# First phase without GpSimd, and adaLN steps issued between the blocks of the second product

## The chip, the cores and the metric

The kernel runs on one core of one Trainium2 chip. The metric is the device time of one launch in microseconds (us). Inputs lie in HBM, the output goes back to HBM, and all arithmetic runs on the core's engines: PE (TensorE), DVE (VectorE), ACT (ScalarE) and POOL (GpSimd). SP issues nearly all loads.

## What is computed

Two layers over 512 latent and 256 context tokens of width 1024. Each layer is a SwiGLU half step, a token mixer and a second SwiGLU half step. Before each of these comes an RMS norm with a shift and a scale, behind it a gate. Cut to what matters here:

```python
for i in range(2):
    mod_l = silu(c)     @ ada_w[i] + ada_b[i]     # 9 vectors of 1024: sh1,sc1,g1, sh2,sc2,g2, sh3,sc3,g3
    mod_c = silu(c_ctx) @ ada_w[i] + ada_b[i]     # the same for the context tokens
    x = x + 0.5 * g1 * swiglu(rms(x) * (1 + sc1) + sh1, pre_wi[i], pre_wo[i])
    x = x + g2 * mixer(rms(x) * (1 + sc2) + sh2)  # attention; layer 0 differential, layer 1 windowed
    x = x + 0.5 * g3 * swiglu(rms(x) * (1 + sc3) + sh3, post_wi[i], post_wo[i])
def swiglu(h, wi, wo):                            # 1024 -> 2 x 2816 -> 1024
    g, u = split(h @ wi); return (silu(g) * u) @ wo
```

The 18 adaLN vectors ("mods") are 18 x 1024 dot products of length 1024 for each of two token types. Their weights, ada_w, are 75 MB.

## The kernel before

Features lie on the 128 partitions, in 8 chunks (d or k); tokens lie on the free axis, 512 latent and 256 context. fp32 matrices are split into two parts, hi and lo (lines 72 to 74: ACT copies the hi part, DVE subtracts it), and each product is the sum of three.

**The four feed-forward steps** (function ffn). The hidden width is 22 slabs f. up(f) makes slab f of the hidden layer: for f = 0, 1, 2 with 8 plain products each (line 522), from f = 3 on with the seven products of a Strassen-Winograd step (line 456). For these, Seven.sums (T1, T2, T3 and their parts) first makes sums and differences of the normalised input (lines 420 to 430), beside up(1) and up(2). After every fourth slab down(g) multiplies four hidden slabs with the second matrix (line 569): 16 blocks, each ended by a DVE instruction that adds it into x (line 390). The last down ends with Norm.follow: squares, sums and the next norm, whose chunks (line 369 on) feed the next product.

**adaLN.** Shift and scale of the first norm (mods 0 and 1 of layer 0) are needed before anything else. For them ada_job reads a 512 KB slab of weights (araw) for each chunk; DVE multiplies and accumulates it for the latent tokens (line 187), POOL multiplies it for the context tokens (line 190) and ACT sums POOL's products (line 199). Four of the eight scale chunks go to PE instead (scale_job, line 215: the weights are the stationary side, 2 columns move). All other mods are made by class Halves in "steps": one step reads 128 x 512 weights (wh, three buffers) and has two accumulating DVE instructions (line 253), one for each type. ffn's hook `beside` issues 6, 4 or 5 of them after each up(f), in the first, second and third feed-forward step.

**Order.** The program is written for a scheduler that orders each engine's instructions beforehand by readiness and program order; keep() pins an instruction to its place in the program. On the chip each engine runs its list strictly in that order, SP its list of loads too.

Of the kernel before, what the change touches and what calls it, by code (L numbers as in the profile page):

```python
# [17 lines left out]
P = 128  # L18
# [24 lines left out]
def hybrid_backbone_kernel(ctx: ExitStack, tc: tile.TileContext, I, out):  # L43
# [74 lines left out]
    def ada_vectors(pool):  # L118

        crep = pool.tile([P, 2, D], F32, name="crep")  # L120
        for ty, nm in enumerate(("c", "c_ctx")):
            nc.sync.dma_start(crep[:, ty], I[nm].partition_broadcast(P))
            nc.scalar.activation(crep[:, ty], crep[:, ty], AF.Silu)
        nc.sync.dma_start(adab, I["ada_b"])
        return crep

    def load_x(half):
        s0, n, _, _ = half
        for d in range(0, KC, 4):
            nc.sync.dma_start(x[:, d:d + 4, s0:s0 + n], I["x"][:, d:d + 4, s0:s0 + n])  # L130
# [42 lines left out]
    JUNK, PRODS = 3, 3  # L173

    def ada_job(l, j, engines, pool, crep, bufs, pin=False):
        m, d = divmod(j, KC)
        w = pool.tile([P, D], F32, name="araw", tag="araw", bufs=bufs)
        nc.sync.dma_start(w, I["ada_w"][l, j])
        if mods[l][m] is None:
            md = const.tile([P, 2, KC], F32, name=f"mod{l}_{m}")  # L180
            mods[l][m] = md[:, 0], md[:, 1], md
        prods = []
        for ty in range(2):
            acc = mods[l][m][ty][:, d:d + 1]
            if engines[ty] is nc.vector:
                o = pool.tile([P, D], BF16, name="junk", tag="junk", bufs=JUNK)
                i = nc.vector.scalar_tensor_tensor(o, w, 1.0, crep[:, ty], ALU.mult, ALU.mult, accum_out=acc)
            else:
                pr = pool.tile([P, D], F32, name="aprod", tag="aprod", bufs=PRODS)
                i = nc.gpsimd.tensor_mul(pr, w, crep[:, ty])  # L190
                prods.append((pr, acc))
            if pin:
                keep(i)
        md = mods[l][m][2][:, :, d]

        def finish():
            for pr, acc in prods:
                o = pool.tile([P, D], BF16, name="junk", tag="junk", bufs=JUNK)
                nc.scalar.activation(o, pr, AF.Identity, accum_out=acc)
            bias = adab[:, l, j:j + 1].broadcast_to([P, 2])  # L200
            if m in (1, 4, 7):
                nc.vector.scalar_tensor_tensor(md, md, 1.0, bias, ALU.add, ALU.add)
            else:
                nc.vector.tensor_add(md, md, bias)
                if m in (2, 8):
                    nc.vector.tensor_scalar_mul(md, md, 0.5)
        return finish

    def scale_job(k, pool, bufs):

        w = pool.tile([P, D], F32, name="araw", tag="araw", bufs=bufs)
        nc.sync.dma_start(w, I["ada_s"][k])
# [3 lines left out]
        bias = adab[:, 0, KC + k:KC + k + 1].broadcast_to([P, 2])  # L216
        return lambda: nc.vector.scalar_tensor_tensor(mods[0][1][2][:, :, k], ps, 1.0, bias, ALU.add, ALU.add)

    class Halves:
# [6 lines left out]
        def add(self, l, ms):  # L226
# [9 lines left out]
            def silu(q):  # L236
                cs = []
                for nm in ("c", "c_ctx"):
                    t = small.tile([P, 512], F32, name="ch", tag="ar", bufs=3)
# [5 lines left out]
            def job(pool, q, m, d):  # L245
# [3 lines left out]
                w = pool.tile([P, 512], F32, name="wh", tag="wh", bufs=3)  # L249
# [11 lines left out]
            for q in range(2):  # L261
                for m in ms:
                    for d in range(KC):
                        def f(pool, q=q, m=m, d=d):
                            if q == 0 and d == 0:
                                bias(m)
                            if m == ms[0] and d == 0:
                                silu(q)
                            job(pool, q, m, d)
                        self.steps.append(f)  # L270

        def __call__(self, n, pool):
            for _ in range(min(n, len(self.steps))):
                self.steps.pop(0)(pool)
# [1007 lines left out]
```

## Time and profile before

| | |
|---|---|
| time, median of 3 runs | 2940.08 us (2938.19 to 2943.32) |
| profiled execution: its own time | 2939.59 us |
| its span, first to last instruction | 2937.8 us |
| PE busy | 2733.8 us (93%) |
| DVE busy | 2229.2 us (76%) |
| ACT busy | 1229.8 us (42%) |
| POOL busy | 498.3 us (17%) |
| mean granted TensorE clock | 0.979 of full |

The profile shows one execution. The time contains 1.8 us outside the span. A busy PE is an upper figure, because matmuls overlap in the records.

### The profile page before, as it was taken

Reading aid. Unit: us, or ns where it says so; the run is one execution under the profiler, and the core shown is the slowest. Engines: PE = TensorE matmul, PEld = TensorE weight load, DVE = VectorE, ACT = ScalarE, POOL = GpSimd, SP = SyncE. Lnnn points to the kernel's source line nnn. Section 1 sums busy time; section 2 is a strip of 40 time slices with the busy share of each in tenths; the row PEclk is TensorE's granted clock in tenths of the full one; section 3 lists DMA queues with packets and bytes.
Section 4 is the critical chain, followed back from the end, with each engine's and each line's share of the span. In section 5 each row is a group of like instructions: output and inputs, shape, how many; then the busy total and the mean of one; then the engine's idle time right before and its main releaser. Section 6 shows DMA issues by size and latency. Waiting matters only on the chain.

```text
span 2937.8 us, 47517 instructions
## 1 busy us (share of the span) xinstructions
PE 2733.8 (93%) x17948; PEld 2589.0 (88%) x17948; DVE 2229.2 (76%) x4613; ACT 1229.8 (42%) x3053; POOL 498.3 (17%) x586
## 2 busy tenths in 40 slices
PE   4799899999999989799999989999999999999999
PEld 3698898889999978789999978999998999999999
DVE  7988987877677756877886598787766766488887
ACT  4423222336556644323333343332334566454443
POOL 5300000025433422200000051000002521220000
PEclk9899999999999999899999999999999999999999
DMA  6333433322011022233332223343322101223333
GB/s 209 114 127 129 133 125 101 119 79 73 30 30 34 26 85 73 86 108 115 109 114 65 72 76 115 126 133 112 100 73 89 45 29 30 73 78 101 98 93 101
DMA packets 98709, 266.49 MB, mean 91 GB/s; under 512 B 12592, under 2 KB 16688, under 8 KB 98352
## 3 DMA queue, kind: packets, MB, share of 16 engines
q1 hardware_dynamic: 91968, 251.78, 26.8%
q10 hardware_dynamic: 6512, 11.68, 1.2%
q8 instruction: 141, 2.31, 0.3%
q14 instruction: 88, 0.72, 0.1%
HBM read 256.07 MB, written 7.34 MB: 90 GB/s over the span
## 4 chain that ended last, share of the span: by engine, by line
PE 66%; DVE 22%; issue 4%; DMA 4%; ACT 2%; POOL 1%; SPq 0%; ACTq 0%; DVEq 0%; POOLq 0%
PE ps_up L456 24%; PE ps_dn L569 22%; PE ps_qkv L651 7%; DVE wlo L74 4%; PE ps_dn L728 4%; DVE wh L253 3%; DVE junkh L253 2%; PE ps_av L989 2%; PE ps_up L522 2%; DMA wh<-in_ada_w 2%; DVE xs L369 1%; DMA raw<-in_pre_wi 1%; PE ps_av L825 1%; PE ps_s L781 1%; PE ps_pt L978 1%
## 5 line engine op out<-in xcount | busy, mean ns | idle before, releaser
L73 ACT CAST whi<-raw 128x512 fp32r<-128x512 f32 x556 | 341.4, 620 | 765.5 <-PE ps_dn L569 318.0
L569 PE MATMUL ps_dn<-ah,whi 128*128 128x256 f32 (+1 forms) x1456 | 463.3, 321 | 2.6 <-DVE x L390 1.8
L74 DVE TENSOR_TENSOR wlo<-raw,whi 128x512 fp32r<-128x512 f32 x556 | 402.9, 729 | 79.9 <-ACT whi L73 68.4
L569 PE MATMUL ps_dn<-al,whi 128*128 128x256 f32 (+1 forms) x1456 | 462.0, 319 | 0.1
L569 PE MATMUL ps_dn<-ah,wlo 128*128 128x256 f32 (+1 forms) x1456 | 454.1, 319 | 0.2 <-DVE wlo L74 0.2
L456 PE MATMUL ps_up<-h_h,whi 128*128 128x384 f32 (+1 forms) x1216 | 400.9, 330 | 38.7 <-ACT whi L73 25.9
L456 PE MATMUL ps_up<-h_h,wlo 128*128 128x384 f32 (+1 forms) x1216 | 394.3, 328 | 12.9 <-DVE wlo L74 12.8
L456 PE MATMUL ps_up<-h_l,whi 128*128 128x384 f32 (+1 forms) x1216 | 397.8, 327 | 0.0
L390 DVE SCALAR_TENSOR_TENSOR x<-ps_dn,mod,x 128x256 f32<-128x256 f32 (+1 forms) x442 | 241.9, 556 | 142.5 <-PE ps_dn L569 101.9
L73 ACT CAST whi<-s 128x512 fp32r<-128x512 f32 x304 | 188.1, 620 | 266.9 <-PE ps_up L456 221.9
L569 PEld LDWEIGHTS ps_dn<-ah,whi 128*128 128x128 f32 x1456 | 276.1, 191 | 25.3 <-ACT whi L73 2.5
L569 PEld LDWEIGHTS ps_dn<-al,whi 128*128 128x128 f32 x1456 | 277.5, 191 | 19.6 <-DVE al L74 0.3
L569 PEld LDWEIGHTS ps_dn<-ah,wlo 128*128 128x128 f32 x1456 | 275.9, 191 | 19.4 <-DVE wlo L74 0.4
L456 PEld LDWEIGHTS ps_up<-h_h,whi 128*128 128x128 f32 x1216 | 233.1, 192 | 47.1 <-ACT whi L73 27.2
L456 PEld LDWEIGHTS ps_up<-h_h,wlo 128*128 128x128 f32 x1216 | 232.2, 192 | 15.1 <-DVE wlo L74 15.0
L74 DVE TENSOR_TENSOR wlo<-s,whi 128x512 fp32r<-128x512 f32 x304 | 208.2, 687 | 41.7 <-ACT whi L73 38.0
L456 PEld LDWEIGHTS ps_up<-h_l,whi 128*128 128x128 f32 x1216 | 233.0, 192 | 0.5
L651 PE MATMUL ps_qkv<-whi,h_h 128*128 128x256 f32 x704 | 205.4, 292 | 4.3 <-DVE a L607 3.6
L651 PE MATMUL ps_qkv<-wlo,h_h 128*128 128x256 f32 x704 | 199.7, 286 | 1.9 <-DVE wlo L74 1.9
L651 PE MATMUL ps_qkv<-whi,h_l 128*128 128x256 f32 x704 | 200.3, 285 | 0.0
L257 POOL TENSOR_TENSOR mod<-mod,part 128x16 f32<-128x16 f32 (+1 forms) x32 | 14.7, 460 | 1065.4 <-DVE wh L253 1031.5
L253 DVE SCALAR_TENSOR_TENSOR wh<-wh,ch 128x512 f32<-128x512 f32 x256 | 185.5, 733 | 1.7 <-DMA wh<-in_ada_w 1.5
(226 smaller groups left out, 6684.9 us busy)
## 6 DMA issues: line engine op xcount, KB each, us to landing
wh<-in_ada_w SPq DMA_DIRECT2D x256, 256.0 KB, 3.7
raw<-in_pre_wi SPq DMA_DIRECT2D x88, 512.0 KB, 3.5
raw<-in_post_wi SPq DMA_DIRECT2D x88, 512.0 KB, 3.5
raw<-in_pre_wo SPq DMA_DIRECT2D x44, 512.0 KB, 3.5
raw<-in_post_wo SPq DMA_DIRECT2D x44, 512.0 KB, 3.5
raw<-in_a_w_qk SPq DMA_DIRECT2D x16, 512.0 KB, 3.5
araw<-in_ada_w SPq DMA_DIRECT2D x12, 512.0 KB, 4.5
raw<-in_a_w_v SPq DMA_DIRECT2D x8, 512.0 KB, 3.5
```

The lines of the kernel that those rows point to most:

```text
L73: nc.scalar.copy(hi, src)
L74: nc.vector.tensor_sub(lo, src, hi.bitcast(F32))
L253: nc.vector.scalar_tensor_tensor(o, w, 1.0, self.c[ty], ALU.mult, ALU.mult, accum_out=self.part[:, ty, d:d + 1])
L369: nc.vector.scalar_tensor_tensor(xs, x[:, d, tk], sc, self.r[p], ALU.mult, ALU.mult)
L390: nc.vector.scalar_tensor_tensor(x[:, d, s0:s0 + n], ps, gate[ty][:, d:d + 1], x[:, d, s0:s0 + n], ALU.mult, ALU.add)
L456: nc.tensor.matmul(ps, ww, z[:, k, :n], start=first and k == 0 and i == 0, stop=k == 3 and i == 2, skip_group_check=True)
L522: nc.tensor.matmul(ps, w, h[:, k, s0:s0 + n], start=k == 0 and i == 0, stop=k == KC - 1 and i == 2)
L569: nc.tensor.matmul(ps, wv, a[:, s0:s0 + n], start=fi == 0 and k == 0, stop=fi == nf - 1 and k == 2)
L651: nc.tensor.matmul(ps, h[:, k, bt], w, start=n == 0, stop=n == 23)
L728: nc.tensor.matmul(ps, wv, o[:, k, s0:s0 + n], start=k == 0 and j == 0, stop=k == KC - 1 and j == 2)
L781: nc.tensor.matmul(sv[:, u], Q[:, c, qt], K[:, c, kb0 * P + u * half:kb0 * P + (u + 1) * half], start=i == 0, stop=i == 1)
L989: nc.tensor.matmul(po[:, j], a[:, k, j], V[:, kb, g], start=k == 0, stop=k == len(kbs) - 1)
```

## The change

- In the first phase the shifts (8 chunks) go to DVE for both token types and the scales (all 8) to PE, with the two columns of cvec as the stationary side and the weights moving, followed by a copy on ACT and a small matmul that turns the row. POOL and ACT's summing leave this phase. The first two shift slabs are loaded ahead of x and summed ahead of the squares; nine araw buffers instead of six.
- Seven.sums and Norm.chunk leave POOL: DVE does the 4 additions and 12 subtractions of a feed-forward step, and the lo parts of chunks 1, 3 and 5 of each norm piece in one fused instruction, with one ACT instruction less each.
- Halves.beside issues 5, 5 and 6 steps after up(0), up(1) and up(2) of the first feed-forward step, none there in the second and third, then one step per up. Halves.between issues 13, 10 and 13 steps over the 16 blocks of each down but the last. The 16 steps of the last mod of layer 0 go behind the blocks of the attention's output product (oproj).

```diff
-    def ada_job(l, j, engines, pool, crep, bufs, pin=False):
...
+    def shift_job(k, pool, crep, bufs):
...
+        keep(nc.sync.dma_start(w, I["ada_w"][0, k]))
+        md = mods[0][0][2][:, :, k]
+
+        def sums():
+            for ty in range(2):
+                o = w if ty else pool.tile([P, D], BF16, name="junk", tag="junk", bufs=2)
+                nc.vector.scalar_tensor_tensor(o, w, 1.0, crep[:, ty], ALU.mult, ALU.mult, accum_out=md[:, ty:ty + 1])
+            nc.vector.tensor_add(md, md, adab[:, 0, k:k + 1].broadcast_to([P, 2]))
+        return sums
...
-        ps = one("ps_a", "acc")[:, :2]
-        for i in range(KC):
-            nc.tensor.matmul(ps, w[:, i * P:(i + 1) * P], cvec[:, i], start=i == 0, stop=i == KC - 1)
...
+            ps = one("ps_a", "acc")
+            for i in range(KC):
+                nc.tensor.matmul(ps[:2, :P], cvec[:, i], w[:, i * P:(i + 1) * P], start=i == 0, stop=i == KC - 1)
+            row = pool.tile([2, P], F32, name="row", tag="row", bufs=2)
+            nc.scalar.copy(row, ps[:2, :P])
+            pt = one("ps_b", "acc")[:, :2]
+            nc.tensor.matmul(pt, row, ident[:2, :2], start=True, stop=True)
...
+        def beside(self, first, early=()):
+
+            def f(i, seven):
+                if i:
+                    self(early[i - 1] if i <= len(early) else int(i > first), (seven.pool, "wh", 3))
+            return f
+
+        def between(self, n):
+
+            def f(i, seven):
+                self((i + 1) * n // 16 - i * n // 16, (seven.pool, "wh", 3))
+            return f
...
-            if d % 2 and d < 7:
-                nc.scalar.activation(xs, xs, AF.Identity, bias=sh)
-                nc.scalar.copy(hi, xs)
-                nc.gpsimd.tensor_sub(lo, xs, hi.bitcast(F32))
-            else:
-                nc.scalar.activation(hi, xs, AF.Identity, bias=sh)
-                nc.vector.scalar_tensor_tensor(lo, xs, sh, hi.bitcast(F32), ALU.add, ALU.subtract)
+            nc.scalar.activation(hi, xs, AF.Identity, bias=sh)
+            nc.vector.scalar_tensor_tensor(lo, xs, sh, hi.bitcast(F32), ALU.add, ALU.subtract)
...
-                    (nc.vector if i else nc.gpsimd).tensor_add(r[:, :2 * n], self.hi[:, kk, :2 * n].bitcast(F32),
+                    nc.vector.tensor_add(r[:, :2 * n], self.hi[:, kk, :2 * n].bitcast(F32),
...
-                    nc.gpsimd.tensor_sub(tl[:, k, :n], t, th[:, k, :n].bitcast(F32))
+                    nc.vector.tensor_sub(tl[:, k, :n], t, th[:, k, :n].bitcast(F32))
...
+            def tick():
+                if between is not None and fs[-1] < NF - 1:
+                    between(next(blocks), seven)
...
-    FIRST = 6
-    ONPE = (2, 3, 4, 6)
...
+    FIRST = 9
...
-    Q0, Q1, Q2 = 6, 4, 5
...
-                halves(Q0, seven.pool)
-        ffn(0, 0, I["pre_wi"][0], I["pre_wo"][0], T, h0, pool, up_done, h1.follow, "right", beside, feed)
+                if f < NF - 1:
+                    others(f, seven)
+        ffn(0, 0, I["pre_wi"][0], I["pre_wo"][0], T, h0, pool, up_done, h1.follow, "right", beside, halves.between(13), feed)
...
-        oproj(0, o.hi, o.lo, I["a_w_o"], T, h2)
+        halves.add(0, (NMOD - 1,))
+        oproj(0, o.hi, o.lo, I["a_w_o"], T, h2, lambda: halves(2, (pool, "st", 5)))
...
-            lambda f, seven: halves(Q1, seven.pool) if 0 < f < NF - 2 else None)
+            halves.beside(3), halves.between(10))
...
-            lambda f, seven: halves(Q2, seven.pool) if 0 < f < NF - 2 else None)
+            halves.beside(3), halves.between(13))
```

The program's order of instructions shows what moved. The first place is DVE's list in the first phase, before the change: L187 are the sums of the first norm's shifts and scales, L1122 multiplies x with the inverse root, L204 and L202 add the bias.

```order
L187 SCALAR_TENSOR_TENSOR junk,mod_0_176<-araw,crep 128x1024
L187 SCALAR_TENSOR_TENSOR junk,mod_1_100<-araw,crep 128x1024
L187 SCALAR_TENSOR_TENSOR junk,mod_0_176<-araw,crep 128x1024
L74 TENSOR_TENSOR wlo<-raw,whi 128x512 x3
L187 SCALAR_TENSOR_TENSOR junk,mod_1_100<-araw,crep 128x1024
L1122 TENSOR_TENSOR xr<-x,rall 128x768 x2
```

And from the start of DVE's list in the changed kernel, where L182 are the shift sums, L1120 adds the squares of x and L201 takes a scale from PE.

```order
L182 SCALAR_TENSOR_TENSOR junk,mod_0_94<-araw,crep 128x1024
L182 SCALAR_TENSOR_TENSOR araw,mod_0_94<-araw,crep 128x1024
L182 SCALAR_TENSOR_TENSOR junk,mod_0_94<-araw,crep 128x1024
L183 TENSOR_TENSOR mod_0_94<-mod_0_94,adab 128x2
L182 SCALAR_TENSOR_TENSOR araw,mod_0_94<-araw,crep 128x1024
L183 TENSOR_TENSOR mod_0_94<-mod_0_94,adab 128x2
L1120 TENSOR_TENSOR xr<-xr 128x512 x5
```

Four shift sums now stand ahead of the squares, no scale sum is left on DVE, and in all 16 such instructions stand where there were 12.

The second place is DVE's list in the first feed-forward step, in up(7), before the change (L253 are the steps; L483, L485 and L487 take products from PE).

```order
L253 SCALAR_TENSOR_TENSOR wh,part<-wh,ch 128x512
L74 TENSOR_TENSOR wlo<-raw,whi 128x512
L483 TENSOR_TENSOR u<-u,ps_up 128x384
L253 SCALAR_TENSOR_TENSOR wh,part<-wh,ch 128x512
L74 TENSOR_TENSOR wlo<-s,whi 128x512
L445 TENSOR_TENSOR s<-raw,s 128x512
L74 TENSOR_TENSOR al<-u,ah 128x384
L253 SCALAR_TENSOR_TENSOR junkh,part<-wh,ch 128x512
L485 TENSOR_TENSOR u<-u,ps_up 128x384
L253 SCALAR_TENSOR_TENSOR junkh,part<-wh,ch 128x512 x2
```

And in the changed kernel the end of the up that stands ahead of the second down; L240 are the steps, L483 and L485 are what L485 and L487 were, and L386 takes the first block of the down.

```order
L483 TENSOR_TENSOR u<-u,ps_up 128x384
L240 SCALAR_TENSOR_TENSOR junkh,part<-wh,ch 128x512
L240 SCALAR_TENSOR_TENSOR wh,part<-wh,ch 128x512
L240 SCALAR_TENSOR_TENSOR junkh,part<-wh,ch 128x512
L240 SCALAR_TENSOR_TENSOR wh,part<-wh,ch 128x512
L74 TENSOR_TENSOR wlo<-raw,whi 128x512
L240 SCALAR_TENSOR_TENSOR wh,part<-wh,ch 128x512
L485 TENSOR_TENSOR u<-u,ps_up 128x384
L74 TENSOR_TENSOR wlo<-raw,whi 128x512
L240 SCALAR_TENSOR_TENSOR junkh,part<-wh,ch 128x512
L386 SCALAR_TENSOR_TENSOR x<-ps_dn,mod_2_735,x 128x512
```

The steps that the program issues between the blocks of a down are drawn ahead by the scheduler, most of them into the up before it: counted from one L475 (L477 before) to the next, the up with the down holds 20 or 22 step instructions and the others 2 to 6, where each held 8 to 13 before, as long as the steps lasted.

The third place is SP's list of loads around the second down, before the change (raw<-in_pre_wi are slabs for an up, raw<-in_pre_wo slabs for a down, wh the weights of the steps).

```order
L94 DMA raw<-in_pre_wi 128x1024
L250 DMA wh<-in_ada_w 128x512 x3
L94 DMA raw<-in_pre_wo 128x1024
L250 DMA wh<-in_ada_w 128x512 x3
L94 DMA raw<-in_pre_wo 128x1024 x3
L94 DMA raw<-in_pre_wi 128x1024 x2
```

And the same place in the changed kernel.

```order
L94 DMA raw<-in_pre_wi 128x1024 x2
L237 DMA wh<-in_ada_w 128x512
L94 DMA raw<-in_pre_wo 128x1024
L237 DMA wh<-in_ada_w 128x512 x3
L94 DMA raw<-in_pre_wo 128x1024
L237 DMA wh<-in_ada_w 128x512 x3
L94 DMA raw<-in_pre_wo 128x1024
```

The three-step groups now stand between the slabs of the down and no longer between those of the ups.

## Rows read from the trace of the kernel before

**Rows 1.** The page: busy time, share and instructions; the chain by engine.
```profile
PE 2733.8 (93%) x17948; PEld 2589.0 (88%) x17948; DVE 2229.2 (76%) x4613; ACT 1229.8 (42%) x3053; POOL 498.3 (17%) x586
PE 66%; DVE 22%; issue 4%; DMA 4%; ACT 2%; POOL 1%; SPq 0%; ACTq 0%; DVEq 0%; POOLq 0%
```

**Rows 2.** Busy time by stretch, its columns first (stretch, length, engines).
```profile
core 0: us, PE busy (x) PEld busy (x) DVE busy (x) ACT busy (x) POOL busy (x), PEclk, DMA share, GB/s
...
90.00:157.00 67.00, 48.35 (x253) 42.89 (x251) 65.64 (x128) 23.30 (x47) 24.39 (x18) 0.85 0.38 115
157.00:620.00 463.00, 436.97 (x2438) 409.60 (x2439) 380.81 (x856) 142.72 (x258) 6.06 (x13) 0.99 0.37 117
620.00:700.00 80.00, 72.66 (x536) 69.55 (x535) 61.16 (x125) 45.72 (x145) 43.54 (x54) 0.98 0.25 87
1040.00:1136.00 96.00, 87.75 (x553) 78.80 (x551) 45.80 (x81) 35.81 (x83) 24.32 (x26) 0.96 0.25 72
1136.00:1230.00 94.00, 74.46 (x410) 66.05 (x409) 87.33 (x162) 41.00 (x88) 34.87 (x28) 0.87 0.28 89
1230.00:1690.00 460.00, 449.68 (x2551) 423.61 (x2552) 343.88 (x698) 148.82 (x272) 6.23 (x12) 1.00 0.31 97
1690.00:1795.00 105.00, 86.83 (x506) 77.54 (x504) 97.81 (x180) 46.83 (x106) 47.82 (x45) 0.90 0.28 90
1795.00:2240.00 445.00, 438.83 (x2498) 415.01 (x2499) 320.44 (x625) 143.87 (x260) 3.65 (x9) 1.00 0.33 106
...
2550.00:2620.00 70.00, 60.72 (x440) 58.82 (x440) 57.56 (x102) 36.24 (x82) 26.34 (x27) 0.88 0.19 61
```

**Rows 3.** The timeline of all engines, 0 to 110 us (start, duration, instruction, idle before).
```profile
22.67 7.58 POOL L190 TENSOR_TENSOR aprod<-araw,crep 128x1024 f32<-128x1024 f32 x3
...
22.88 2.05 PE L303 MATMUL ps_r<-dg,ones 128*128 128x512 f32 x2 [1.16 <-DVE dg L295]
...
27.97 3.36 DVE L187 SCALAR_TENSOR_TENSOR junk<-araw,crep 128x1024 bf16<-128x1024 f32 x1
...
29.12 3.41 PE L215 MATMUL ps_a<-cvec,araw 128*128 128x2 f32 x16
...
31.27 1.21 DVE L187 SCALAR_TENSOR_TENSOR junk<-araw,crep 128x1024 bf16<-128x1024 f32 x1
```

**Rows 4.** DVE's timeline, 72 to 170 us.
```profile
83.50 0.95 DVE L1136 TENSOR_TENSOR h_l<-xr,h_h 128x768 fp32r<-128x768 f32 x1
84.37 0.69 DVE L253 SCALAR_TENSOR_TENSOR junkh<-wh,ch 128x512 bf16<-128x512 f32 x1
84.98 0.08 DVE L253 DVE_READ_ACCUMULATOR junkh<-wh,ch 128x1 f32 x1
...
103.39 2.20 DVE L426 TENSOR_TENSOR t<-both 128x384 f32<-128x384 f32 x1
...
115.29 0.55 DVE L426 TENSOR_TENSOR t<-both 128x384 f32<-128x384 f32 x1
...
156.75 0.55 DVE L477 TENSOR_TENSOR u<-u,ps_up 128x384 f32<-128x384 f32 x1
```

**Rows 5.** POOL's groups by shape: total busy, mean ns, idle before.
```profile
L373 POOL TENSOR_TENSOR h_l<-xs,h_h 128x256 fp32r<-128x256 f32 x42 | 35.0, 833 | 33.4 <-ACT h_h L372 31.5 <-PE ps_up L522 1.3
L190 POOL TENSOR_TENSOR aprod<-araw,crep 128x1024 f32<-128x1024 f32 x12 | 34.3, 2881 | 13.5 <-ACT junk L199 13.5
...
L420 POOL TENSOR_TENSOR both<-h_h,h_l 128x768 f32<-128x768 f32 x12 | 26.4, 2209 | 5.6 <-DVE t L426 3.8 <-DVE mod L217 1.8
...
L430 POOL TENSOR_TENSOR T1l<-t,T1h 128x384 fp32r<-128x384 f32 x12 | 16.6, 1387 | 54.7 <-ACT T1h L429 54.7
```

**Rows 6.** PE's timeline in an up, 268 to 300 us.
```profile
267.67 0.34 PE L456 MATMUL ps_up<-T1l,whi 128*128 128x384 f32 x1
...
268.02 0.34 PE L456 MATMUL ps_up<-T3l,whi 128*128 128x384 f32 x1
```

**Rows 7.** The page's loads: instruction, count, size, median us to landing.
```profile
raw<-in_pre_wi SPq DMA_DIRECT2D x88, 512.0 KB, 3.5
```

More of the change, by code (lines that the diff above doesn't have):

```diff
@@ L219, in hybrid_backbone_kernel @@
+        return sums
     class Halves:
@@ L394, in into_x @@
                             follow(p, d)
+                    if tick is not None:
+                        tick()
     class Seven:
@@ L498, in hybrid_backbone_kernel, with ffn @@
     EARLY = 1
-    def ffn(l, msh, w1, w2, nt, norm, pool, after_up, follow, side, beside=None, feed=None):
+    def ffn(l, msh, w1, w2, nt, norm, pool, after_up, follow, side, beside=None, between=None, feed=None):
         seven = None
@@ L574, in down @@
             for group in ([jobs] if last else [[j] for j in jobs]):
-                into_x(group, parts_of(nt) if last else halves, mods[l][msh + 2], product, follow if last else None)
+                into_x(group, parts_of(nt) if last else halves, mods[l][msh + 2], product, follow if last else None,
+                       tick)
         for f in range(NF):
@@ L720, in finish, with oproj @@
                 self.tick()
-    def oproj(l, oh, ol, w, nt, norm):
+    def oproj(l, oh, ol, w, nt, norm, tick=None):
         def product(ps, wt, i, d, s0, n):
@@ L732, in oproj @@
             into_x([(w[d], [d]) for d in ds], parts_of(nt) if len(ds) > 1 else halves_of(nt), mods[l][5], product,
-                   norm.follow)
+                   norm.follow, tick)
     def diff_attention(norm, O, pool, save, finish_proj, ready):
@@ L1094, in hybrid_backbone_kernel @@
     nc.scalar.activation(cvec, cvec, AF.Silu)
-    crep = ada_vectors(start)
-    md = const.tile([P, 2, KC], F32, name="mod0_1")
-    mods[0][1] = md[:, 0], md[:, 1], md
+    for m in range(2):
+        md = const.tile([P, 2, KC], F32, name=f"mod0_{m}")
+        mods[0][m] = md[:, 0], md[:, 1], md
     with tc.tile_pool(name="f0", bufs=1) as pool:
         load_small()
+        crep = ada_vectors(start)
+        shifts = [shift_job(k, start, crep, FIRST) for k in range(2)]
+        keep(nc.sync.dma_start(adab, I["ada_b"]))
         for hf in range(2):
             load_x(all_[hf])
+        scales = [scale_job(k, start, FIRST) for k in range(2)]
+        for f in shifts:
+            f()
         xr = [pool.tile([P, T], F32, name="xr", tag=("ah", "al")[d % 2], bufs=5) for d in range(KC)]
@@ L1136, in feed @@
             nc.vector.tensor_sub(lo, xr[k], hi.bitcast(F32))
-            for f in rest.pop(k + 1, ()):
+            for f in later.get(k + 2, ()):
                 f()
-        vectors(0)
-        vectors(1)
         h1 = Norm(0, 3, T, "right", "h1_")
@@ L1146, in hybrid_backbone_kernel @@
         halves.add(0, (2,))
-        halves.add(0, range(3, NMOD))
+        halves.add(0, range(3, NMOD - 1))
+        others = halves.beside(3, (5, 5, 6))
         def beside(f, seven):
```

84 lines of the change are left out of this document (25 added, 59 removed).

## The prediction

> **What bounds the kernel now.** I read the page's busy line and its chain first. PE is busy for 93% of the span and holds 66% of the chain, DVE for 76% and 22% [rows 1]. So the kernel is bound by PE, and only the stretches where PE stands still can give anything. Next I read the busy times by stretch [rows 2]; a stretch's loss is its length less PE's busy time, and on top of that the busy time at the low clock (busy time times one minus the granted clock, which is below 1 in just the stretches where PE stands idle). Up to 157 us PE gets little done. In 90 to 157 it is busy for 48.35 of 67 us, and DVE for 65.64. In 157 to 620, the ups and downs of the first feed-forward step, 26 us are lost beside 381 us of DVE. The same stage is nearly clean in the second and third feed-forward step (10.3 and 6.2 us lost). The sums stages ahead of them are not: 1136 to 1230 loses 19.5 us and 1690 to 1795 loses 18.2, at a granted clock of 0.87 and 0.90, and DVE is busy for 87 of 94 and 98 of 105 us. The reader is to see one pattern: PE waits where DVE is full, and POOL is busy in the same stretches (24, 35 and 48 us).
>
> Third, why DVE is full. Its timeline shows one instruction at two prices. The same L426 takes 0.55 us at 115.29 and 2.20 at 103.39 [rows 4]; L187 takes 1.21 us at 31.27 and 3.36 at 27.97, when POOL's three products from 22.67 to 30.25 still run [rows 3]. Without POOL beside it one instruction starts 0.87 us after a 768-wide one (83.50 to 84.37) and 0.61 after a 512-wide accumulating one (84.37 to 84.98) [rows 4]; with the same overlap of 0.08 a 384-wide one costs 0.47 and a 1024-wide accumulating one 1.13. I price DVE's lists by these steps (0.60, 0.41 and 0.33 for 512, for the fused 256 and for the plain 256, in proportion).
>
> **The change, part by part.**
>
> *First phase and first sums stage, 0 to 157.* DVE's list from its first add to the first L477 comes to 96.5 us by these steps. The changed list has four more shift sums (4.6 us), four additions (3.5) and twelve subtractions (5.6) from POOL, and seven step instructions fewer (4.3): 105.9 us. At 22.7 us, where POOL's products begin [rows 3], DVE before the change has about 88 us of its list ahead and reaches L477 only at 156.75 [rows 4]: 134 us for 88, so 46 are lost to POOL and to waiting. In the changed list four sums (4.6) fall into the time before x is there. x lands behind two more 512 KB slabs; one alone takes 3.5 us [rows 7], so the same point comes some 3.5 us later, at 26, with 94 us ahead (105.9 less 4.6 and some 7 of adds). POOL's 34.3 us of products [rows 5] are gone; waits remain, since PE now does three scale jobs ahead of the second half of the root. A job in the new form is in no row: by the 512-wide fp32 matmul of 2.05 us [rows 3], a quarter of it eight times, 4.1 us; before, a job's eight matmuls, x16 in the records, took 3.41 us [rows 3]. I take 4.1 and half of that as the other end, and 8 us of waits for DVE in all. That makes 26 + 94 + 8 = 128, and PE has its work for this time. **27 us less** (ends: 12 if the waits are 23, 38 if there are none).
>
> *First feed-forward step, 157 to 620.* A step is two instructions, 1.22 us of DVE. An up costs DVE 11 instructions of 512 and 9 of 384, 10.8 us; with the 12 step instructions of before, 18.1. PE needs 84 matmuls, one each 0.175 us [rows 6], 14.7 us. So each up was 3.4 us over, and the down repaid it. Afterwards three ups of four hold 2 to 6 step instructions, 12.0 to 14.5 us: under 14.7. The fourth holds some 17 ahead of the down's first block: 10.8 + 10.4 = 21.2, 6.5 over. There DVE is about three products ahead (3 x 2.1 us), which covers most of it. I count 2 us for each of five downs, take them from the 26 lost [rows 2], and not all of these were due to steps: **12 us less** (ends: 22 less; 7 more, if nothing covers 5 x 6.5).
>
> *Sums stage of the second feed-forward step, 1136 to 1230.* Behind oproj's last block DVE's list is 67.8 us; the changed one lacks 29 step instructions (17.7) and has 9 fused chunk instructions (3.7), 3.5 and 5.6 from POOL's sums, less some small ones: 61.7. DVE was busy for 87; the excess goes with POOL. PE's own work, 74.46 us of which some is at the lower clock, then bounds the stage. 19.5 idle and 0.13 x 74 = 9.7 of low clock are there to have; the norm's handover at its start stays. **16 less** (8 to 24). *The third*, 1690 to 1795: list 62.0 to 56.9 us, 18.2 idle and 8.7 of clock: **14 less** (6 to 22).
>
> *Ups and downs of the second and third:* 16.5 us lost [rows 2], up to 18 step instructions in the up ahead of a down. **6 less** (11 less to 14 more).
>
> *Norm pieces and the last sums stage.* 42 pieces leave POOL (35.0 us [rows 5]) and an ACT copy each; DVE gains 42 x 0.41 = 17 us where it was full, and loses POOL's company (26.4 and 16.6 us and more in the sums [rows 5]). In 620 to 700 PE loses 7.3 us, in 2550 to 2620 9.3 and 7.3 of clock. **3 less** (10 less to 8 more).
>
> *The 16 steps in oproj:* 19.5 us of DVE where it is busy for 45.8 of 96 [rows 2]; the idle half hides them, without it they would cost up to 6. **1 more.**
>
> Sum: -27 - 12 - 16 - 14 - 6 - 3 + 1 = -77, from the profiled execution's 2939.6: 2863. That execution lies 0.5 us under the median.
>
> **Two rules.** The rows show DVE slowed up to four times while POOL works [rows 3, 4]. The Trainium skill, "SBUF — State Buffer", section "Who interferes with whom", says that a DVE instruction with two SBUF inputs and a GpSimd one that reads SBUF exclude each other, each for the whole instruction; by it POOL's work costs DVE as much as doing it, and the sum is the one above or a little better. Against the change stands "Perfetto Trace Analysis", section "Optimizing Scalar/DVE Operations", of the Trainium skill: a saturated DVE is to be unloaded, to Scalar or even GpSimd (though it adds that between those two it might not help). By it the sum would be the third rival's.
>
> **Rivals.**
> 1. *The wait moves into the last up before a down.* All 17 step instructions delay the seven products: 6.5 us at five downs, and the second and third steps pay their upper ends: -77 + 19 + 20 = -38, 2902. For it: DVE runs its list strictly, and the list has the bunch. Against: the prefetch.
> 2. *More is won:* the first phase, both sums stages and the first ups near their best ends, -105: 2835.
> 3. *POOL is not what slows DVE* (slower than before). Then the 46 us of the first phase stay on a longer list: 26 + 94 + 46 = 166, 9 more. The sums stages give 4 each from the missing steps, the last one costs 6, the norms 8, oproj 1, the ups give 6: 10 more, 2950. It decides from the point where less than an eighth of the excess is POOL's doing (10 against the 87 us between this case and the forecast). Against it is the coincidence in [rows 3].
> 4. *SP's queue.* Three pinned step loads stand between a down's slabs, and each waits for a buffer that DVE frees. If a slab came 2.5 us late, 45 times (15 downs, 3 slabs): 112 more, 2975; from 1.7 us on it is slower. Against: the steps run an up ahead, and so do the loads.
>
> **How the numbers follow.** Forecast 0.68 (2840 to 2888 by itself), rival 1 0.15, rival 2 0.05, rival 3 0.07, rival 4 0.05. The range 2836 to 2905 leaves out rivals 3 and 4, half of rival 2 and edges of the others. A measurement of this kernel can tell 0.2%, 6 us. Faster: 0.68 + 0.15 + 0.05 and a little of rival 3, 0.90; same 0.03; slower 0.07.
>
> **What would show it.** In the changed profile: first L475 on DVE near 128 us, no 768- or 384-wide DVE instruction of the sums over 1 us; PE losing under 16 us in the ups and downs of the first step; both sums stages with a granted clock above 0.95. Rival 1 would show PE waits of 5 us on lo parts or u at each first block of a down; rival 3 slow DVE instructions without POOL; rival 4 DVE and ACT waiting for raw in the downs. I am wrong if DVE's waits in the first phase exceed 23 us, since that term is the largest.

## Result, and the profile after

| | before | changed |
|---|---|---|
| median, us | 2941.7 (2938.2 to 2944.2, 4 runs) | 2841.4 (2838.1 to 2851.8, 4 runs) |
| profiled execution: span, mean granted clock | 2937.8, 0.98 | 2838.1, 0.99 |

The ratio is 0.9666 with an interval of 0.9638 to 0.9694: 98 us less (90 to 106). Forecast were 77 less, 2863; the range 2836 to 2905 holds the time. The two profiled executions differ by 99.6 us. The page of the changed kernel, its busy line and its chain by engine:

```profile
PE 2701.7 (95%) x18028; PEld 2561.8 (90%) x18028; DVE 2185.6 (77%) x4727; ACT 1207.4 (43%) x2999; POOL 343.8 (12%) x468
PE 73%; DVE 14%; DMA 5%; ACT 3%; issue 2%; POOL 1%; SPq 0%; ACTq 0%; POOLq 0%; DVEq 0%
```

Against [rows 1], DVE's share of the chain fell from 22% to 14% and PE's rose from 66% to 73%, while DVE is as busy as before: 114 instructions more, 44 us less. Busy time by stretch, the columns as in [rows 2]:

```profile
73.00:134.00 61.00, 44.94 (x247) 39.99 (x245) 59.03 (x136) 22.41 (x46) 1.22 (x3) 0.86 0.39 120
134.00:573.00 439.00, 430.44 (x2439) 406.43 (x2440) 366.28 (x808) 144.17 (x260) 4.59 (x10) 0.99 0.37 117
573.00:650.00 77.00, 69.82 (x503) 66.86 (x502) 58.82 (x130) 39.75 (x129) 36.44 (x45) 0.96 0.26 90
1080.00:1160.00 80.00, 76.83 (x502) 70.42 (x501) 66.50 (x139) 37.75 (x81) 4.89 (x6) 0.98 0.21 61
1094.40:1160.50 66.10, 62.93 (x395) 56.52 (x394) 61.74 (x128) 34.64 (x75) 1.97 (x2) 1.00 0.22 66
1603.00:1702.00 99.00, 92.59 (x597) 85.24 (x596) 85.87 (x173) 50.55 (x109) 17.30 (x21) 0.98 0.20 61
1702.00:2137.00 435.00, 431.89 (x2460) 408.68 (x2459) 329.62 (x671) 143.68 (x259) 4.91 (x11) 1.00 0.37 118
2450.00:2520.00 70.00, 64.11 (x487) 62.30 (x485) 55.42 (x126) 35.08 (x80) 5.04 (x6) 0.93 0.25 76
```

The first feed-forward step (134 to 573) loses 8.6 us of PE, where it lost 26. The sums stages of the second and third step (1080 to 1160, 1603 to 1702) lose 3.2 and 6.4 at a granted clock of 0.98, where they lost 19.5 and 18.2 at 0.87 and 0.90. The row from 1094.40 begins, as 1136 to 1230 in [rows 2] does, behind the projection's last matmul; the row from 1080 holds 14 us of the projection too. The first sums stage (73 to 134) is still DVE's: 59.03 of 61 us. DVE's timeline there and ahead of it:

```profile
38.07 1.22 DVE L182 SCALAR_TENSOR_TENSOR araw<-araw,crep 128x1024 f32<-128x1024 f32 x1
...
62.12 0.16 DVE L201 SCALAR_TENSOR_TENSOR mod<-ps_b,adab 128x2 f32<-128x2 f32 x1 [4.40 <-PE ps_b L199]
64.52 0.96 DVE L1139 TENSOR_TENSOR h_l<-xr,h_h 128x768 fp32r<-128x768 f32 x1 [2.24 <-ACT h_h L1138]
66.57 0.16 DVE L201 SCALAR_TENSOR_TENSOR mod<-ps_b,adab 128x2 f32<-128x2 f32 x1 [1.09 <-PE ps_b L199]
68.97 0.96 DVE L1139 TENSOR_TENSOR h_l<-xr,h_h 128x768 fp32r<-128x768 f32 x1 [2.24 <-ACT h_h L1138]
...
83.63 0.55 DVE L424 TENSOR_TENSOR t<-both 128x384 f32<-128x384 f32 x1
...
134.41 0.55 DVE L475 TENSOR_TENSOR u<-u,ps_up 128x384 f32<-128x384 f32 x1
```

The subtraction that took 2.20 us in [rows 4] is L424 now and takes 0.55; a shift sum takes 1.22 where it took 3.36 in [rows 3]. The last `h_l` starts at 68.97 instead of 83.50 and the first L475 at 134.41 instead of 156.75. In brackets stands what bounds the end of the first phase now: scale job on PE, copy on ACT, back to PE and DVE, scaling on ACT, the hi part on ACT, `h_l` on DVE, one after the other, and DVE idle between.

To see where time goes in every kernel below, I cut its span at one instruction of DVE's timeline: the first and the last start of the addition `u<-u,ps_up` (L477 before, L475 after; the last row above is the first such start) in each of the four feed-forward steps. That addition takes the first pair of an up's products, so "first pair" below is its first start in the program; "step 1" to "step 4" are the feed-forward steps, a step without a number is one of adaLN. A second profiled execution of the changed kernel (after_again) differs from the first by up to 3 us in a row of this table. Differences to the profiled execution of before, in us (e1 to e4 are the first four runs below):

```
                     before   changed  e1     e2     e3     e4
0 to first, step 1    156.8   -22.3   -18.5   -0.6   -4.2  -19.5
step 1, first-last    462.9   -24.4    +3.6  -23.4   +3.3  -21.9
to first of step 2    610.5   -22.9    -0.6  -17.3   -7.8  -12.2
step 2                442.3    -0.4    -2.1   +0.4   +0.6   -0.8
to first of step 3    122.5   -22.8    +1.2  -18.3   -4.4  -18.3
step 3                434.8    -0.4    -0.3   +1.2   -0.2   +0.9
to first of step 4    390.0    -6.7     0.0   +1.6   -4.2   +1.0
step 4                295.2    +0.4    +0.4   +0.9   -0.3   +1.0
```

### The profile page after: what moved, and what is told of

It is laid out like the page before. It is cut to its first block, busy times and chain, and to the rows that moved or that the text cites. A ratio compares the mean times of both kernels' runs of the same rounds, so it can differ in the third digit from the quotient of the medians.

```text
span 2838.1 us, 47439 instructions
## 1 busy us (share of the span) xinstructions
PE 2701.7 (95%) x18028; PEld 2561.8 (90%) x18028; DVE 2185.6 (77%) x4727; ACT 1207.4 (43%) x2999; POOL 343.8 (12%) x468
## 4 chain that ended last, share of the span: by engine, by line
PE 73%; DVE 14%; DMA 5%; ACT 3%; issue 2%; POOL 1%; SPq 0%; ACTq 0%; POOLq 0%; DVEq 0%
PE ps_up L454 26%; PE ps_dn L568 22%; PE ps_qkv L657 7%; PE ps_up L521 5%; PE ps_dn L734 4%; DMA wh<-in_ada_w 3%; DVE wlo L74 2%; PE ps_av L995 2%; DVE wh L240 1%; DMA raw<-in_pre_wi 1%; PE ps_av L831 1%; PE ps_s L787 1%; DVE xs L369 1%; PE ps_pt L984 1%; DVE junkh L240 1%
## 5 line engine op out<-in xcount | busy, mean ns | idle before, releaser
L568 PE MATMUL ps_dn<-ah,whi 128*128 128x256 f32 (+1 forms) x1456 | 464.6, 322 | 12.4 <-DVE x L386 10.7
L74 DVE TENSOR_TENSOR wlo<-raw,whi 128x512 fp32r<-128x512 f32 x556 | 383.0, 693 | 77.2 <-ACT whi L73 59.6
L454 PE MATMUL ps_up<-h_h,whi 128*128 128x384 f32 (+1 forms) x1216 | 396.6, 326 | 23.0 <-ACT whi L73 16.5
L386 DVE SCALAR_TENSOR_TENSOR x<-ps_dn,mod,x 128x256 f32<-128x256 f32 (+1 forms) x442 | 240.6, 554 | 129.6 <-PE ps_dn L568 104.8
L240 DVE SCALAR_TENSOR_TENSOR wh<-wh,ch 128x512 f32<-128x512 f32 x256 | 173.8, 690 | 19.5 <-DMA wh<-in_ada_w 19.3
```

The lines of the kernel that those rows point to most:

```text
L74: nc.vector.tensor_sub(lo, src, hi.bitcast(F32))
L240: nc.vector.scalar_tensor_tensor(o, w, 1.0, self.c[ty], ALU.mult, ALU.mult, accum_out=self.part[:, ty, d:d + 1])
L386: nc.vector.scalar_tensor_tensor(x[:, d, s0:s0 + n], ps, gate[ty][:, d:d + 1], x[:, d, s0:s0 + n], ALU.mult, ALU.add)
L454: nc.tensor.matmul(ps, ww, z[:, k, :n], start=first and k == 0 and i == 0, stop=k == 3 and i == 2, skip_group_check=True)
L568: nc.tensor.matmul(ps, wv, a[:, s0:s0 + n], start=fi == 0 and k == 0, stop=fi == nf - 1 and k == 2)
```

## Experiments

**The change in three parts, and one part undone.** Three kernels hold one part each; together they are the change. The theory behind the prediction (A) is that POOL beside DVE cost DVE its time; the rival (B) is that the steps' places did.

Run e1_first_phase: the kernel before with `shift_job`, `scale_job` and the new first phase alone.

> The kernel before with the first part of the change alone: shifts on DVE, scales on PE, no POOL product in the first phase; the steps keep their old places and POOL its part of the sums and the norms. Theory A (POOL beside DVE is what cost DVE its time): the first phase gains its 20 us and more, but the first sums stage keeps POOL's additions and subtractions, so the first product pair's add comes near 140 us and the time falls by 14 to 20 us, all of it before 160 us. Theory B (the steps' places are what mattered): the first phase gains at most the 5 us by which its own DVE list is shorter, under 8 us in all. Under both nothing changes behind the first feed-forward step's sums.

2923.8 us, ratio 0.9938 (0.9925 to 0.9952): 18.9 less, first pair at 138.3. As A has it, though this kernel also takes four scales' sums off DVE; e7_pool_first_phase below tells the two apart.

Run e2_steps_moved: the kernel before with `beside`, `between` and the steps in the output projection alone.

> The kernel before with the steps' new places alone (16 in the first sums stage instead of 12, one beside three ups of four, 13 or 10 between a down's blocks, 16 in the first output projection, none in the second and third sums stages); first phase, sums and norms as before, with POOL. Theory A: the first feed-forward step gains its 24 us, but the second and third sums stage only what 29 and 25 step instructions cost DVE without POOL's company, 0.6 us each, half of it on the path: 5 to 9 us each. Total 34 to 42 us less. Theory B: both sums stages gain nearly all of their 23 us, total 62 to 72 us less.

2887.2 us, 0.9814 (0.9798 to 0.9830): 55.5 less, between the theories and nearer to B. The first step gained its 23.4; the two sums stages gained 17.3 and 18.3, twice to three times what I expected under A. Twenty-six step instructions left the third sums stage. In the kernel before they and their accumulator reads are busy there for 21.2 us with POOL beside them; by the undisturbed 0.61 of [rows 4] they take 16. So their whole undisturbed price had been on the path; my "half of it on the path" was wrong.

Run e3_sums_norm_dve:

```diff
-  (nc.vector if i else nc.gpsimd).tensor_add(r[:, :2 * n], ...
+  nc.vector.tensor_add(r[:, :2 * n], ...
-  nc.gpsimd.tensor_sub(tl[:, k, :n], ...
+  nc.vector.tensor_sub(tl[:, k, :n], ...
```

and the norm's lo parts likewise.

> The kernel before with the sums and the norm's lo parts all on DVE; first phase and steps as before. Theory A: DVE's list grows by some 17 us for the norms and 9 us for each sums stage, but loses POOL's company: second and third sums stage 12 to 16 us less each, the first 5, the last 4, total 30 to 42 us less. Theory B: the lists are longer where DVE is full already, so the sums stages lose 5 us each and the time is 5 to 20 us more. The third rival of the prediction (POOL is not what slows DVE) is theory B here.

2922.8 us, 0.9939 (0.9925 to 0.9952): 19.9 less. A has the sign, at about half its size; B and the prediction's third rival have the wrong sign. DVE got longer lists in the places where it was full, and these places got shorter.

Run e4_after_pool_back: the changed kernel with the edit of e3_sums_norm_dve undone.

> The changed kernel with POOL back in the sums and in the norm's lo parts (three of eight); first phase and steps as changed. Theory A: the sums stages of the second and third feed-forward step give back 12 to 16 us each, the first and the last 5 each: 34 to 42 us above the changed kernel. Theory B: the sums stages keep their gain, within 8 us of the changed kernel. If the parts add up, this kernel stands where the gains of the first two runs together stand.

2869.5 us, 0.9752 (0.9739 to 0.9766): 28 above the changed kernel, where A had 34 to 42 and B at most 8. The second and third sums stage give back 10.7 and 4.5, where A had 12 to 16 each. The kernel stands where the gains of the first two runs stand together (73.2 against 18.9 + 55.5). All three parts sum to 94 of the 100 by medians; in the table most of the difference lies in step 1, where the three parts give 16.5 together and the change 24.4 (21.6 in its second execution). Of the 3.6 and 3.3 us by which e1 and e3 lengthen step 1, little is seen where the steps are moved as well (e4, changed); why is open. DVE by operation in the third sums stage, with POOL back (e4_after_pool_back, 1618 to 1722; columns: busy, mean ns | idle before):

```profile
L74 DVE TENSOR_TENSOR wlo<-raw,whi 128x512 fp32r<-128x512 f32 x19 | 16.3, 868 | 0.7 <-ACT whi L73 0.6
L391 DVE SCALAR_TENSOR_TENSOR x<-ps_dn,mod,x 128x256 f32<-128x256 f32 x24 | 10.9, 477 | 2.0 <-PE ps_dn L573 1.4
...
L427 DVE TENSOR_TENSOR t<-both 128x384 f32<-128x384 f32 x4 | 3.8, 956 | 1.4 <-POOL both L423 1.4
...
L559 DVE TENSOR_TENSOR sg<-sg,ps_up 128x512 f32<-128x512 f32 x3 | 2.0, 675 | 0.0
```

and in the changed kernel (1602 to 1702):

```profile
L74 DVE TENSOR_TENSOR wlo<-raw,whi 128x512 fp32r<-128x512 f32 x19 | 12.8, 689 | 0.3 <-ACT whi L73 0.3
...
L386 DVE SCALAR_TENSOR_TENSOR x<-ps_dn,mod,x 128x256 f32<-128x256 f32 x24 | 10.9, 477 | 2.0 <-PE ps_dn L568 1.4
...
L422 DVE TENSOR_TENSOR t<-both 128x384 f32<-128x384 f32 x4 | 2.2, 543 | 0.0
...
L554 DVE TENSOR_TENSOR sg<-sg,ps_up 128x512 f32<-128x512 f32 x3 | 2.0, 675 | 1.6 <-PE ps_up L521 1.6
```

The reader is to see which rows move. Instructions with two inputs in SBUF do (956 to 543 ns, 868 to 689); those that take one input from PSUM (`ps_dn`, `ps_up`) don't, to the nanosecond, though 18 of the 24 additions into `x` run beside a POOL instruction with POOL back.

**POOL's presence by itself.** Three kernels add POOL work that nobody waits for to the changed kernel; no list of DVE's changes.

Run e5_pool_reads (second and third sums stage):

```diff
+  if self.dummy:
+      scr = self.pool.tile([P, 512], F32, name="wh", tag="wh", bufs=3)[:, :384]
+      nc.gpsimd.tensor_copy(scr[:, :1], self.T[0][0][:, k, :1].bitcast(F32))
+      for j in range(5):
+          nc.gpsimd.tensor_add(scr, x[:, j, :384], x[:, j + 1, :384])
```

> The changed kernel with twenty additions of 384 elements on POOL in the sums stage of the second and of the third feed-forward step each, of two SBUF inputs, whose result nobody reads; DVE's list is that of the changed kernel. Theory A (POOL's reading of SBUF stops DVE): POOL is busy for some 26 us more in each stage; in the kernel with POOL put back, 34 us of POOL's work drew DVE's same instructions out by 19 us (384-wide additions from 0.54 to 0.93 us), so 15 us of DVE here, and with the 13 us per stage in which DVE now stands free 5 to 10 us per stage: 10 to 20 us in all. Theory C (what cost time was only that DVE and PE waited for POOL's late results): no change, under 3 us.

Run e6_pool_writes: `for j in range(10): nc.gpsimd.memset(scr, 0.0)` in place of the additions.

> As the run with POOL additions, but forty memsets of 384 elements at the same places, which write the same tiles and read nothing. Theory A with exclusion only for reading: DVE's 384-wide instructions stay at 0.54 us and the time is that of the changed kernel within 3 us. Rival (any POOL work in SBUF slows DVE): 384-wide instructions above 0.7 us, 5 us and more.

2873.8 us (0.9764, 0.9748 to 0.9780) and 2843.3 us (0.9664, 0.9645 to 0.9683). POOL's row and two of DVE's in the third sums stage of the run with additions (1618 to 1733):

```profile
L436 POOL TENSOR_TENSOR wh<-x 128x384 f32<-128x384 f32 x20 | 33.2, 1666 | 1.1
...
L427 DVE TENSOR_TENSOR t<-both 128x384 f32<-128x384 f32 x4 | 4.6, 1154 | 0.0
...
L562 DVE TENSOR_TENSOR sg<-sg,ps_up 128x512 f32<-128x512 f32 x3 | 2.0, 675 | 0.0
```

and of the run with memsets (1601 to 1702):

```profile
L436 POOL MEMSET wh<- 128x384 f32 x40 | 16.6, 420 | 2.0
...
L434 POOL COPY wh<-T1h 128x1 f32<-128x1 f32 x4 | 11.7, 2934 | 18.2 <-ACT T1h L430 18.2
...
L427 DVE TENSOR_TENSOR t<-both 128x384 f32<-128x384 f32 x4 | 2.2, 540 | 0.0
```

Reading costs, writing doesn't: 1154 against 540 ns for the same instruction. With the additions DVE is busy in that stage for 102.67 us, 16.3 more than in the changed kernel, near the 15 I expected; but the two stages became longer by 15.1 and 13.6 us against the run with memsets, 30.5 us in all by medians where A had 10 to 20. The 13 us that DVE stands free there are no cushion: in 7.5 of them it waits for PE, in 3.9 for ACT. The copy of a single column in the memset run takes 2.9 us on average, 0.19 (at 1689.79) with no DVE instruction beside it and 7.67 (at 1670.89) beside 17 of them in a row, so POOL's reads wait for DVE too. The Trainium skill, "SBUF — State Buffer", section "Who interferes with whom", says that a DVE instruction with two SBUF inputs contends with a GpSimd instruction that reads SBUF, not with one that only writes it, and that one with at most one SBUF input outside DVE's 2-port modes doesn't contend; all of these rows agree.

Run e7_pool_first_phase: 24 unread 512-wide products on POOL in `feed`, beside one column copied from `mod`; one `junk` buffer less.

> The changed kernel with 24 products of 512 elements on POOL in the first phase (the twelve 1024-wide ones of before, cut in halves), results unread, and one buffer less for the junk output. DVE is idle for 13 of the 53 us from 20 to 73 us, so theory A expects: POOL busy some 34 us more, the shift sums and scalings beside it at two to three times their time, and the first pair's add 8 to 16 us later than 134 us. Theory C (the first phase gained because four scales' sums and finishing copies left the list): under 3 us.

2856.5 us, 0.9704 (0.9688 to 0.9721): 13.2 above the run with memsets, the first pair at 145.3, 11 later. DVE's timeline:

```profile
51.56 0.94 DVE L1140 TENSOR_TENSOR h_l<-xr,h_h 128x768 fp32r<-128x768 f32 x1
52.43 2.29 DVE L182 SCALAR_TENSOR_TENSOR araw<-araw,crep 128x1024 f32<-128x1024 f32 x1
54.65 0.08 DVE L182 DVE_READ_ACCUMULATOR araw<-araw,crep 128x1 f32 x1
54.65 2.29 DVE L182 SCALAR_TENSOR_TENSOR junk<-araw,crep 128x1024 bf16<-128x1024 f32 x1
56.87 0.08 DVE L182 DVE_READ_ACCUMULATOR junk<-araw,crep 128x1 f32 x1
56.87 2.03 DVE L1140 TENSOR_TENSOR h_l<-xr,h_h 128x768 fp32r<-128x768 f32 x1
58.83 1.25 DVE L183 TENSOR_TENSOR mod<-mod,adab 128x2 f32<-128x2 f32 x1
```

The DVE instructions that are held up here are longer by nearly one fixed amount (1.22 to 2.29, 0.95 to 2.03, and the addition of two elements, 0.15 alone, to 1.25: 1.1 each), whatever their own length, as if each waited out one POOL product (1.27 us where it runs alone). Not every one beside a product is: the first `h_l` above is not. So by this stand-in about half of the first phase's 22 us is POOL's company (11); that the rest is what else that part of the change does is inferred.

**What bounds it now.** Run e8_gates_early: five columns of the first gate summed like shifts, in `feed`; `GATES` is (3, 4, 5, 6, 7).

```diff
+            if k + 1 in GATES:
+                gates[k + 1] = gate_job(GATES.index(k + 1), start, crep, FIRST)
...
+            if k in gates:
+                gates[k]()
-        others = halves.beside(3, (5, 5, 6))
+        others = halves.beside(3, (2, 2, 2))
```

> The changed kernel with five of the eight columns of the first gate summed in the first phase (1024-wide pairs on DVE, four instructions a column, between 50 and 70 us, where DVE is idle for 12 us and the DMA queue for 23), so six steps instead of sixteen stand in the first sums stage. If that stage (73 to 134 us, DVE busy for 59 of 61) is bound by DVE's list, ten steps less take 12 us off it, and the time falls by 8 to 12 us below the changed kernel, first pair's add near 124 us. Rival: PE's own work or the late end of the first phase bounds it, and the sums added in the first phase delay the last products by up to 12 us: no change or 3 us more.

2839.5 us, 0.9652 (0.9635 to 0.9670). The first pair came at 124.1, as expected, so the first sums stage is bound by DVE's list; but step 1 took 445.3 us instead of 438.4 (441.3 in the second execution), for which I have no cause, and the whole is 3.8 under the run with memsets on the same chip, no difference that can be told.

Run e9_oproj_free: no steps in the output projection, two an up in step 1.

```diff
-        others = halves.beside(3, (5, 5, 6))
+        others = halves.beside(3, (5, 5, 6), 2)
-        oproj(0, o.hi, o.lo, I["a_w_o"], T, h2, lambda: halves(2, (pool, "st", 5)))
+        oproj(0, o.hi, o.lo, I["a_w_o"], T, h2)
```

> The changed kernel without steps in the first output projection: its sixteen steps stand beside the ups of the first feed-forward step, two an up instead of one. In the changed kernel PE waits 7.6 us in that projection for lo and hi parts that stand behind steps on DVE and behind gain loads; before it waited for none. Theory: these waits are the steps' price, which the prediction put at 1 us; they go, and two steps an up (10.8 + 2.4 us of DVE under 14.7 of PE) cost nothing: 5 to 8 us less than the changed kernel, the stretch from the first step's last pair to the second step's first near 581 us. Rival: the waits come from the gain loads alone, which stay: within 2 us of the changed kernel.

Run after_again:

> The changed kernel itself, on the same chip as the runs beside it: 2841 us, ratio 0.966 to 0.967, so that differences of a few us can be told.

2849.1 us (0.9680, 0.9662 to 0.9698) and 2843.9 us (0.9662, 0.9645 to 0.9680): no gain, where I had 5 to 8 us less. Waits of PE and of its weight loads (PEld) in the output projections of the changed kernel's second run, which the run without steps doesn't have at all:

```profile
its engine sat idle before it (us, times) until:
  DVE wlo L74: 5.5, 3
  issue: 3.6, 1
  DVE x L386: 3.4, 1
```

The stretch with the projection became 6.5 us shorter (589.3 to 582.9), as expected, and the projection itself, from its first to its last matmul, 83.7 to 74.3 us (74.0 before the change). The gain loads stayed, so the rival fell: these are the steps. But step 1 became 8.2 us longer; two steps an up are not free. Its groups of four ups and a down, from one first-pair addition to the next, show where a step costs (step instructions and us in the three intervals without the down, in the one with it, and us of the group; "changed" is its first execution):

```
                  second group                 fourth group
               ups       down     sum       ups       down     sum
changed     12, 43.8   22, 48.8   92.6   12, 44.3   20, 48.4   92.7
e9          19, 48.0   23, 47.6   95.6   19, 48.0   19, 46.6   94.7
before      36, 51.9   12, 47.6   99.6   36, 53.3    0, 45.9   99.1
```

In the fourth group the kernel before has fewer step instructions than e9 (36 against 38) and takes 4.4 us more: not their number counts but how many stand in the ups. In e9 the scheduler put 7, 2 and 10 into the three ups, not four each. Busy time in the second group's two parts, before and in the changed kernel (columns as in [rows 2]):

```profile
214.80:266.80 52.00, 46.96 (x255) 45.23 (x254) 52.00 (x129) 18.11 (x33) 1.43 (x3) 0.97 0.44 144
266.80:314.40 47.60, 47.60 (x275) 43.73 (x274) 35.60 (x74) 13.13 (x24) 0.00 (x0) 1.00 0.33 110
...
193.30:237.10 43.80, 43.56 (x250) 42.93 (x249) 38.47 (x82) 18.61 (x35) 0.60 (x1) 1.00 0.35 111
237.10:285.90 48.80, 48.80 (x282) 44.85 (x281) 40.33 (x93) 12.33 (x23) 0.83 (x2) 1.00 0.39 122
```

Before, DVE is busy for all of the ups and PE is not, and POOL works there for 1.4 us only: in the ups the steps fill DVE, not POOL. In the changed kernel PE is busy for 92.4 of 92.6 us: neither the steps left beside the ups nor the bunch around the down make it wait in this group.

Run e11_all_three: e8_gates_early and e9_oproj_free together, and the small loads of `load_gains` and `load_rest` issued on SP behind the seventh `feed`.

> Three moves together on the changed kernel: five gate columns summed in the first phase, no steps in the first output projection, and the small loads and table work for the attention, which stood beside the eighteenth up of the first feed-forward step (its interval was 20 to 22 us, the others 13 to 16), issued on SP in the first phase, where SP's queue is empty from 43 to 66 us. If each takes its own wait away: 4 for the gates, 5 to 8 for the projection, 4 to 6 for the eighteenth up, 13 to 18 us below the changed kernel. Rival: PE, busy for 95% of the span, takes most of it back, or the table load for the exponential on ACT lands on the first phase's tail: 0 to 6 us less.

2841.3 us, 0.9652 (0.9635 to 0.9669): 2.6 under the changed kernel beside it, as the rival had it. The eighteenth up's interval fell from 21.1 to 14.9, but the first pair came at 130.8, not 124, and step 1, with two steps an up as in e9, took 446.5 us.

Run e12_loads_in_downs: e8_gates_early, the steps in the projection as in the changed kernel, and

```diff
-                if f == 17:
-                    load_gains(0, "a")
-                    load_rest(small)
+            if blocks[0] == 2 * 16 + 4:
+                load_gains(0, "a")
+            if blocks[0] == 3 * 16 + 4:
+                load_rest(small)
```

> The run with the gates early, and in place of the eighteenth up the gains' loads and tables stand at the fourth block of the third down and the other small loads at that of the fourth, where ACT and DVE run ahead of PE; nothing new in the first phase. Theory (two waits taken away, neither given back): first pair at 124 us, the eighteenth up back from 21 to 15 us, 8 to 10 us below the changed kernel's 2842. Rival (the wait only moves: the small loads block ACT and DVE in the down for the same 6 us and PE is as late): 2839, as with the gates alone.

2828.9 us, 0.9615 (0.9602 to 0.9628): 12 to 15 under the two medians of the changed kernel, and the interval of the ratio overlaps with neither of its two. That is more than the 8 to 10 expected. First pair at 126.9, three later than expected, the eighteenth up at 14.2, step 1 in 433.6 us. This version beats both kernels. The move of the small loads was not run without the early gates, so how much each gives is not shown; the group with the eighteenth up fell from 99.5 us in the changed kernel, and 100.5 with the gates alone, to 91.0. The first stretches, 73 to 100 and 100 to 127:

```profile
73.00:100.00 27.00, 27.00 (x155) 23.48 (x154) 26.28 (x57) 12.96 (x26) 0.91 (x2) 1.00 0.44 148
100.00:127.00 27.00, 20.75 (x105) 19.44 (x104) 22.98 (x46) 11.82 (x25) 0.44 (x1) 0.87 0.17 49
```

PE is busy for all of the first stretch and idle for 6.3 us of the second, the most that is still to be won there beside the clock of 0.87.

## Why the prediction was right, and where it was off

The sign and the reading (PE waits where DVE is full, DVE is full because POOL stops it and steps stand in its list) held. Of the two causes the steps' places are the larger: 55.5 us by themselves, against 19.9 for the sums and norms and 18.9 for the first phase, of which about 11 is POOL's company. Of what was to show it, three of four came: no long sums instruction on DVE, 8.6 us lost in the first step, both clocks at 0.98; the first L475 did not come at 128. The time lies nearer to the second rival's 2835 than to the forecast, by its mechanism: sums stages and first ups at their best ends or beyond, though not the first phase. Four terms were too small by 37 us in all and three too large by 17; that the range still holds the time, 5 us from its end, owes something to this.

- *First phase and first sums stage:* 27 forecast, 22.3 measured; first L475 at 134.4, not 128 (128 is 28.75 less than 156.75; the sum took 27). The 8 us of waits for DVE were mis-sized: it is idle for 13 of the 53 us from 20 to 73, 5.5 of them until scales come from PE and 6.6 until ACT has made the hi parts with them, and for 2 of the 61 behind. A scale job was priced at 2 to 4.1 us and took 1.9 to 3.6. POOL's part is shown by a stand-in (e7_pool_first_phase).
- *First step:* 12 forecast, 24.4 measured, the largest error. The step that failed is "the down repaid it", with the 26 us taken as the most there was and the 2 us for each down. In the second group the ups were 8.1 us longer before than in the changed kernel and the down's interval 1.2 shorter: hardly anything was repaid. The bunch around the down, for which I took off 2 us, leaves PE busy throughout. And the gain is 17 us of the 26 lost (8.6 are left) and 7 us of PE's own busy time, 437 before and 430 now, which the 26 did not contain. "Under 14.7" held: such ups now run at PE's pace (43.8 us for three). The steps' places are what did it (e2_steps_moved gains 23.4 with nothing else changed).
- *Sums stages of the second and third step:* 16 and 14 forecast. Behind the projection's last matmul the second became 28.2 us shorter (94.3 to 66.1), beyond the best end of 24; the 22.9 of the table has the longer projection in it. The third gained 22.8, its best end being 22. The causes were right, and DVE's list too (61.7 forecast, 61.74 busy). In the table the parts alone give 17.3 and 18.3 for the steps, 7.8 and 4.4 for POOL. Mis-sized was what stays: I left 13 of 29 us of idle time and low clock standing in the second, and 3.2 are left, at a clock of 1.00 (6.4 at 0.98 in the third). Ahead of step 1's first pair the granted clock is 0.86 now and PE is idle for 16 of 61 us; in the ups and downs it is 0.99 and 1.00.
- *Ups and downs of the second and third step:* 6 forecast, 0.8 measured. Their steps were four or five an up before, not six; that this left little wait to take away is argued, not tested.
- *Norm pieces and last sums stage:* 3 forecast; the stretch up to step 4's first pair alone gave 6.7, and it is POOL's leaving that gave it (e3_sums_norm_dve 4.2 by itself, e4_after_pool_back none of it).
- *Steps in the projection:* 1 forecast; 6.5 measured by the stretch (e9_oproj_free) and 8 to 9 by the projection alone (82.1 and 83.7 us against 74.3), above the upper end of 6. That DVE is idle for half of that stretch did not hide them: PE waits there for lo parts and `x` from DVE, whose list has the steps between them.
- *Rival 1* (the wait moves into the last up) exists, small: PE waits for `x` in the downs for 10.7 us in all, longest 3.0, against 39 in the rival's sum and the 5 us it was to show at each. *Rival 3* fell with e3_sums_norm_dve and e5_pool_reads. *Rival 4* was not seen: in step 1 of the repeated run ACT waits once, for 0.9 us, for a down's slab (5.1 us before the change).

By "Perfetto Trace Analysis", section "Optimizing Scalar/DVE Operations", of the Trainium skill, offloading some work of a saturated DVE to Scalar or even GpSimd may make sense, a weaker word than the prediction's, but between DVE and GpSimd it might not help. That doubt decided here: 25 instructions more on DVE in the third sums stage and 4.2 us less of busy time (90.59 with POOL back in e4_after_pool_back, 86.40 without).

## What to carry to other kernels

Where one instruction of DVE shows two prices in a trace, look for POOL work with SBUF inputs beside it before unloading DVE further; doing that work on a full DVE can be a gain. Price filler work in an in-order list by the place where it stands, not by the engine's idle time on average: here its full length where DVE is full (the third sums stage, 26 step instructions, 18.3 us), a third to a half of it where DVE is idle for half of the stretch (the projection, 19.5 us of steps, 6.5 to 9), and next to nothing around a down, where PE's own work lasts longer. A loss read as length less PE's busy time is no upper bound for what can be won: that busy time fell too. And when a wait is taken away early in a program, measure the whole: a move that brought the first pair forward by 10 us gained 2 to 4 by itself, too little to be told, and 12 to 15 together with another move (the small loads).

## What the runs showed of the hardware

A DVE instruction that is held up by a POOL product is not slowed in proportion: it is longer by 1.07, 1.08 and 1.10 us for lengths of 1.22, 0.95 and 0.15 (e7_pool_first_phase). POOL waits in turn: its copy of one column took 0.19 us alone and 7.67 beside 17 DVE instructions in a row (e6_pool_writes). And a stage paid for it nearly in full (16.3 us more of DVE, 13.6 us more time), although DVE had 13 us idle in it (e5_pool_reads).
